# A hybrid decoder layer on one core: pages in VectorE's waits, a third sequence's values on VectorE, norm sums as float32r products, weight loads by groups

## The chip, the core and the metric

The kernel runs on one core of a Trainium2 chip. The metric is device time in microseconds (us), the median of repeated runs. TensorE multiplies matrices, VectorE and ScalarE work elementwise, GpSimd takes small elementwise work, SyncE issues DMAs. ScalarE's queue issues DMAs too.

## What is computed

One inference step of one layer. 512 prompt tokens, 16 meta tokens and 8 new tokens of 8 running sequences are normed and projected by one weight matrix, `w_in` (2048 x 8192). Its columns feed 8 heads of a gated recurrence (HGRN2) and 8 heads of differential attention. Each head's output is normed over its 128 values and gated, and `w_out` (2048 x 2048) maps the result back. The 8 new tokens also attend to 2048 cached positions each, in 16 pages of 128 rows for keys and 16 for values per sequence:

```python
z = rmsnorm(h, norm_g) @ w_in                    # split into hq, hf, hi, hg, aq, ak, av, ag
# new tokens: for each of 8 sequences, over 16 pages
s = einsum('bqhcd,bkhcd->bchqk', q, k) * 64 ** -0.5 + bias   # c = 0, 1: two key halves of 64
p = softmax(s); w = p[:, 0] - lam * p[:, 1]
o_at = einsum('bhqk,bkhv->bqhv', w, v)
# merge
mixed = concat(rmsnorm(o_hg) * silu(hg), rmsnorm(o_at) * silu(ag))
y = rmsnorm(h + mixed @ w_out)
```

Everything is float32, outputs included.

## The kernel before

**Projections.** The weights go through in 80 blocks of 128 columns, 64 of `w_in` (aq, ak, av, then hi/hf/hq by heads, hg, ag) and 16 of `w_out`. A block is four groups (`NG = 4`), each of four 128x128 weight tiles (`GK = 4`), so there are 320 groups, numbered u. Each operand is kept as two float32r parts: ScalarE casts the weights to `hi`, VectorE subtracts to get `lo` (`split`, L322). A group is 24 products on TensorE (`group`, L337): hi by xh, hi by xl and lo by xh, for two halves of the tokens, accumulated in `ps`. `split(u + LEAD)` runs three groups ahead; `hi` and `lo` have four buffers each, `ps` three.

**Weight loads.** `load_raw` (L314) loads half a block, 512 KB, into one of three `raw` buffers. After the first three, ScalarE's queue issues them, at every second group, behind that group's `hi` cast; the buffer must have been read by the `lo` of an earlier group.

**Around the groups.** The loop over u (L1317) emits `split`, `group`, then at a block's end `block_done` (ScalarE evacuates `ps`), then one step of each waiting thread: `attn` (L910), `hgrn` (L998), `norm_chain` (L875) for a head's norm, `softmax_dec` (L777) for the weights of one sequence, and so on. Then `value_step` and `fill`. Everything is recorded by `Counted`, so that all calls show line L151 and are best told apart by tiles. Each engine runs its own queue in the order in which the calls are emitted.

**Pages.** `page_step` (L675) does one half of a key page on VectorE: a product with the query (`pgt<-pgt,qb`), then a sum by heads (`scd<-pgt`). 128 key pages go before the last values may. Values of sequences 0 to 5 are weighted on TensorE (`value_step`, L702): eight steps for a sequence, each two pages, four products `t_pv<-pgt,wd`, added up on VectorE (`acc`). Sequences 6 and 7 (`ONV`, L282) go on VectorE (`dve_value_step`, L733): eight fused multiply-adds `qb<-pgt,wd,qb` for a page, and at the end two products with a matrix of ones on TensorE (`pv_sum`, L761).

**What sets the order.** `Clock` keeps an estimate of each engine's time while the program is written. `fill` (L603) emits page steps as long as VectorE's estimate is less than TensorE's plus `LATE`, which depends on the phase (before values, attention, recurrence, after):

```python
LATE, SOON = (3.0, 1.5, 4.0, 4.0), 0.0
while clock["dve"] < clock["pe"] + LATE[ph]:
    ...
    if not page_step() and not dve_value_step():
        break
```

At group 253 the program stops emitting groups until all norms and all values are done (L1327); any step that is still left stands there, between two groups.

**Norms of a head.** `norm_chain` squares a head's 512 tokens on ScalarE, sums over the partitions by one float32 product with ones (`t_ra` for attention, `t_rh` for the recurrence; 16 in all), and scales. The `tp` buffers of PSUM, two of them, are shared by nearly all of TensorE's small work.

**DMAs.** The DMAs of both issuing queues take eight completion semaphores (DMAHW0 to DMAHW7) in turn. A DMA whose semaphore is still in use by the DMA eight before it waits for that one to land, in its issuing queue.

Of the kernel before, what the change touches and what calls it, by code (L numbers as in the profile page):

```python
# [18 lines left out]
P = 128  # L19
D = 2048  # L20
# [55 lines left out]
class Clock:  # L76
# [30 lines left out]

    def issue(self, e, cost, outs, ins, latency=0.08, shared=False):
        start = self.now[e]
        for table, aps in ((self.written, ins + outs), (self.read, outs)):  # L110
            for ap in aps:
                t, by = table.get(ap.tensor.name, (0.0, e))
                if by != e:
                    start = max(start, t + self.LATENCY)
        if e == "pool":
            start = self.port(start)
            self.pool_held = start + cost
        elif shared:
            start = max(start, self.pool_held)
            a, b = self.held[-1]  # L120
            self.held = self.held[-40:]
            if start - b < 0.03:
                self.held[-1] = (a, start + cost)
            else:
                self.held.append((start, start + cost))
        self.now[e] = end = start + cost
        end += latency
        for ap in ins:
            n = ap.tensor.name
            self.read[n] = max(self.read.get(n, (0.0, "")), (end, e))  # L130
        for ap in outs:
            self.written[ap.tensor.name] = end, e
# [7 lines left out]

class Counted:


    def __init__(self, eng, clock, name):
        self.eng, self.clock, self.name = eng, clock, name

    def __getattr__(self, op):
        f = getattr(self.eng, op)

        def call(*a, **k):  # L150
            r = f(*a, **k)  # L151
            aps = [x for x in a if hasattr(x, "free_size")]
            outs = [x for x in (k.get("out"), k.get("accum_out")) if x is not None]
            if "out" not in k:
                outs.append(aps.pop(0))
            ins = aps + [x for n, x in k.items() if hasattr(x, "free_size") and n not in ("out", "accum_out")]
            n = max(ins[0].free_size(), 1) if op == "tensor_reduce" else (outs[-1] if "out" not in k else outs[0]).free_size()
            late, shared = 0.08, False
# [39 lines left out]
def layer_kernel(ctx: ExitStack, tc: tile.TileContext, A):  # L198
# [67 lines left out]
    load_x(1)  # L266
    ones = cp.tile([P, P], F32, name="ones")
    G.memset(ones, 1.0)
    eps = cp.tile([P, 1], F32, name="eps")
# [11 lines left out]
    NKB, NPB = 3, 2  # L281
    ONV = (6, 7)  # L282
    NG = KC // GK
    LEAD = 3

# [28 lines left out]
    def load_raw(i):  # L314

        b, z = divmod(i, 2)
        if b < NB:
            raws[i] = wp.tile([P, KC // 2, P], F32, name="raw", tag="raw", bufs=3)
            clock.arrive(raws[i], 0.5)
            (store if i > 2 else load)(out=raws[i], in_=blocks[b][1][z * D // 2:(z + 1) * D // 2, :].rearrange("(k p) n -> p k n", p=P))  # L320

    def split(u):  # L322

        if u >= NB * NG:
            return
        b, g = divmod(u, NG)
        i, z = divmod(u, NG // 2)
        raw = raws[i][:, z * GK:(z + 1) * GK, :]
        hi = clock.tile(wp.tile([P, GK, P], F32R, name="hi", tag="hi", bufs=4), "hi", 4)
# [3 lines left out]
        parts[u] = (hi, lo)  # L333
        if z == 0 and i:
            load_raw(i + 2)

# [17 lines left out]

    load_raw(0)


# [27 lines left out]

    load_x(2)
    load_raw(1)
    load_x(3)
    load_raw(2)
    norm_stat(4)  # L390
# [160 lines left out]

    for g in range(NG):
        split(NG + g)
# [27 lines left out]
    def flag(name):  # L581
        flags[name] = slot[0]
# [17 lines left out]

    LATE, SOON = (3.0, 1.5, 4.0, 4.0), 0.0

    def fill():  # L603

        ph = 0 if "av0" not in flags else 1 if "attn7" not in flags else 2 if "hgrn7" not in flags else 3
        while clock["dve"] < clock["pe"] + LATE[ph]:
            if turn_v[0] and dve_value_step():
                turn_v[0] = 0
                continue
            i = done[0]  # L610
            if i < len(kloaded) and any(clock.written[t.tensor.name][0] > clock["pe"] + SOON for t in (kloaded[i], qbs[ksteps[i][0]])):
                if not dve_value_step():
                    break
                continue
            turn_v[0] = 1
            if not page_step() and not dve_value_step():
                break

# [208 lines left out]
    def decode_q():  # L827
# [9 lines left out]
        load_values()  # L837
        flag("q")
        yield

# [34 lines left out]
    def norm_chain(o, n, g, name, sq=None):  # L875

        if sq is None:
            sq = hw.tile([P, 512], F32, name="sq", tag="t6")[:, :n]
        S.activation(sq, o, AF.Square)
        yield  # L880
        t = tp("t_" + name)
        T.matmul(t[:, :n], ones, sq, start=True, stop=True)
        S.activation(sq, t[:, :n], AF.Ln, scale=1.0 / P, bias=eps)
# [26 lines left out]
    def attn():  # L910
        live = {}
        for n in range(4 * H + 4):
# [53 lines left out]
            if i2:  # L966
# [5 lines left out]
                V.tensor_scalar(r[:, 1:2], r[:, 1:2], nlam, None, op0=ALU.mult)  # L972
                S.activation(p1[:, :L1], p1[:, :L1], AF.Copy, scale=r[:, 1:2])
            fill()
            if i2:
                V.scalar_tensor_tensor(p0[:, :L1], p0[:, :L1], r[:, 0:1], p1[:, :L1], op0=ALU.mult, op1=ALU.add)
            if n < 4 * H:
# [427 lines left out]
```

## Time and profile before

| | us |
|---|---|
| median of 3 runs | 1261.57 (1259.65 to 1262.13) |
| the profiled execution | 1256.73 |
| its span in the trace | 1254.9 |
| TensorE busy (matmuls) | 1214.3 |
| VectorE busy | 844.9 |
| ScalarE busy | 547.8 |

The granted clock averages 0.994 over the span. The span goes by stages: up to 40 us the prompt is normed and transposed, to 150 us groups alone, to 240 us groups beside key pages, to 450 us attention heads beside groups, to 880 us the recurrence, to 1020 us gates beside values, then `w_out`. A row of the list of waits names the instruction that waited, what it waited for, us in total, times and the longest. A row of the timeline gives start, duration, engine, line and operation, with the idle time before it in brackets.

### The profile page before, as it was taken

The page shows a single profiled execution, that of the slowest core. Times are in us where ns is not written, and L with a number is a line of the kernel's source. Part 1 is how long each engine was busy: PE and PEld are TensorE (multiplying, and loading weights), DVE is VectorE, ACT ScalarE, POOL GpSimd, SP SyncE. Part 2 cuts the span into 40 slices and gives each one's busy share as a digit, 9 for nine tenths or more (in the row PEclk, how much of TensorE's full clock was granted, in tenths as well). Part 3 has the DMA queues.
Part 4 walks back from the last instruction along what each step waited for, and adds up shares of the span by engine and source line. Part 5 has one row for each costly group of instructions (what it writes and reads, how often), then busy time and mean ns, then how long its engine had stood idle before and what let it go on. Part 6 is the DMA issues. An engine that isn't in the chain of part 4 may idle for free.

```text
span 1254.9 us, 24952 instructions
## 1 busy us (share of the span) xinstructions
PE 1214.3 (97%) x9412; PEld 1096.5 (87%) x9412; DVE 844.9 (67%) x1527; ACT 547.8 (44%) x1288; POOL 144.7 (12%) x151
## 2 busy tenths in 40 slices
PE   8999999999999999999998999999999999999995
PEld 6899999976777779888787888888999999999995
DVE  6522598865666578878668788888997936355253
ACT  6322323355555664545445455554432235223233
POOL 2000001100000001111012010122131410021020
PEclk9999999999999999999999999999999999999998
DMA  7353788935645576889796897987787636433223
GB/s 230 95 161 97 239 275 283 285 103 189 191 163 188 183 234 190 297 272 305 256 318 193 296 307 256 323 286 247 226 287 226 204 101 217 122 89 96 86 68 137
DMA packets 240956, 261.02 MB, mean 208 GB/s; under 512 B 8783, under 2 KB 198962, under 8 KB 240171
## 3 DMA queue, kind: packets, MB, share of 16 engines
q1 hardware_dynamic: 57298, 164.09, 37.5%
q10 hardware_dynamic: 183538, 95.34, 26.9%
q8 instruction: 74, 1.21, 0.4%
q14 instruction: 46, 0.38, 0.1%
HBM read 245.94 MB, written 16.14 MB: 209 GB/s over the span
## 4 chain that ended last, share of the span: by engine, by line
PE 86%; DVE 5%; DMA 4%; ACT 3%; issue 1%; ACTq 1%; SPq 0%; DVEq 0%
PE ps L151 69%; PE t_pv L151 4%; PE o L151 2%; PE ho L151 2%; PE sc L151 1%; DMA raw<-in_w_out 1%; DMA pgt<-in_cache_v 1%; DVE qb L151 1%; PE up L151 1%; PE t_w L151 1%; DVE lo L151 1%; PE at L151 1%; DVE scd L151 1%; PE t_ra L151 1%; PE t_y L151 1%
## 5 line engine op out<-in xcount | busy, mean ns | idle before, releaser
L151 PE MATMUL ps<-xh,hi 128*128 128x264 f32 (+2 forms) x2048 | 539.2, 294 | 3.9 <-ACT gate L151 2.2
L151 PE MATMUL ps<-xl,hi 128*128 128x264 f32 (+2 forms) x2048 | 521.8, 285 | 1.1 <-DVE xl L151 1.1
L151 PEld LDWEIGHTS ps<-xh,hi 128*128 128x128 f32 x2048 | 386.7, 189 | 58.2 <-issue 48.2
L151 PEld LDWEIGHTS ps<-xl,hi 128*128 128x128 f32 x2048 | 386.8, 189 | 2.6 <-issue 2.5
L151 DVE TENSOR_TENSOR lo<-raw,hi 128x512 fp32r<-128x512 f32 x321 | 244.1, 765 | 198.9 <-ACT hi L151 198.3
L151 PE MATMUL ps<-xh,lo 128*128 128x264 f32 (+2 forms) x2048 | 333.8, 285 | 0.0
L151 ACT CAST hi<-raw 128x512 fp32r<-128x512 f32 x321 | 196.3, 617 | 228.7 <-PE ps L151 187.5
L151 PEld LDWEIGHTS ps<-xh,lo 128*128 128x128 f32 x2048 | 284.6, 189 | 0.0
L151 DVE TENSOR_TENSOR pgt<-pgt,qb 128x1024 f32<-128x1024 f32 x128 | 163.7, 1279 | 14.5 <-DMA pgt<-in_cache_k 11.3
L151 DVE TENSOR_REDUCE scd<-pgt 128x16 f32<-128x1024 f32 x128 | 155.0, 1211 | 0.1
L151 PE MATMUL ps<-mh,hi 128*128 128x256 f32 (+1 forms) x512 | 130.0, 286 | 0.5 <-ACT y L151 0.5
L151 PE MATMUL ps<-ml,hi 128*128 128x256 f32 (+1 forms) x512 | 128.5, 283 | 0.0
L151 PEld LDWEIGHTS ps<-mh,hi 128*128 128x128 f32 x512 | 96.4, 188 | 1.0 <-ACT y L151 0.7
L151 PEld LDWEIGHTS ps<-ml,hi 128*128 128x128 f32 x512 | 96.5, 188 | 0.0
L151 PE MATMUL ps<-mh,lo 128*128 128x256 f32 (+1 forms) x512 | 82.5, 283 | 0.0
L151 DVE SCALAR_TENSOR_TENSOR qb<-pgt,wd,qb 128x128 f32<-128x128 f32 x240 | 70.9, 364 | 0.0
L151 PEld LDWEIGHTS ps<-mh,lo 128*128 128x128 f32 x512 | 70.3, 188 | 0.0
L151 PE MATMUL t_pv<-pgt,wd 128*32 128x512 f32 x384 | 53.9, 605 | 12.7 <-ACT wmT L151 4.2
L151 DVE SCALAR_TENSOR_TENSOR p<-p,r,p 128x144 f32<-128x144 f32 (+3 forms) x32 | 18.2, 568 | 71.3 <-ACT p L151 71.2
L151 DVE TENSOR_TENSOR acc<-acc,t_pv 128x512 f32<-128x512 f32 x42 | 28.7, 682 | 23.9 <-PE t_pv L151 23.9
L151 POOL TENSOR_TENSOR sd<-sd,vb 128x1024 f32<-128x1024 f32 x8 | 20.1, 2509 | 183.4 <-ACT vb L151 156.5
L151 ACT COPY hgm<-ho 128x128 f32<-128x128 f32 x32 | 8.5, 265 | 69.5 <-PE ho L151 59.6
(242 smaller groups left out, 1167.2 us busy)
## 6 DMA issues: line engine op xcount, KB each, us to landing
pgt<-in_cache_k SPq DMA_DIRECT2D x128, 512.0 KB
pgt<-in_cache_v SPq DMA_DIRECT2D x128, 512.0 KB
raw<-in_w_in ACTq DMA_DIRECT2D x125, 512.0 KB
raw<-in_w_out ACTq DMA_DIRECT2D x32, 512.0 KB
x<-in_x_prompt SPq DMA_DIRECT2D x4, 1024.0 KB
qb<-qd SPq DMA_DIRECT2D x8, 512.0 KB
sd<-in_state_hgrn SPq DMA_DIRECT2D x8, 512.0 KB
vb<-hvd SPq DMA_DIRECT2D x8, 512.0 KB
```

The costliest lines, as they stand in the source:

```text
L151: r = f(*a, **k)
```

## The change

- A VectorE instruction that would wait over 1 us by the estimate first lets page steps be emitted, as long as the wait lasts (`meanwhile`); `LATE` goes down in all four phases.
- Sequence 5's values are done on VectorE too (`ONV`).
- The 16 norms of heads: ScalarE squares into a `tp` buffer, casts to `sqh`, VectorE subtracts (`rest`), and two float32r products with ones replace the float32 one.
- Weights are loaded by groups of 256 KB into five buffers, one load at each group.
- In attention, the scaling of the second softmax half (`p<-p,r`) goes from ScalarE to VectorE, behind `fill`.
- The ones are cast to float32r on GpSimd at the start; one split that was done twice is done once.

```diff
--- before.py
+++ after.py
@@ Clock, Counted @@
+    def ready(self, e, outs, ins):
+
+        start = 0.0
         for table, aps in ((self.written, ins + outs), (self.read, outs)):
...
+        return start
+
+    def issue(self, e, cost, outs, ins, latency=0.08, shared=False):
+        start = max(self.now[e], self.ready(e, outs, ins))
...
 class Counted:
+    WAIT = 1.0
...
+            if self.meanwhile:
+                step, self.meanwhile = self.meanwhile, None
+                while self.clock.ready(self.name, outs, ins) - self.clock[self.name] > self.WAIT and step():
+                    pass
+                self.meanwhile = step
+            r = f(*a, **k)
@@ layer_kernel @@
-    ones = cp.tile([P, P], F32, name="ones")
-    G.memset(ones, 1.0)
+    ones_f = hw.tile([P, P], F32, name="ones_f", tag="ones")
+    G.memset(ones_f, 1.0)
+    ones_r = cp.tile([P, P], F32R, name="ones")
+    G.tensor_copy(ones_r, ones_f)
+    ones = ones_r.bitcast(F32)
...
-    ONV = (6, 7)
+    ONV = (5, 6, 7)
     NG = KC // GK
+    NRAW = 5
@@ load_raw, split @@
-        b, z = divmod(i, 2)
+        b, z = divmod(i, NG)
         if b < NB:
-            raws[i] = wp.tile([P, KC // 2, P], F32, name="raw", tag="raw", bufs=3)
-            clock.arrive(raws[i], 0.5)
-            (store if i > 2 else load)(out=raws[i], in_=blocks[b][1][z * D // 2:(z + 1) * D // 2, :].rearrange("(k p) n -> p k n", p=P))
+            raws[i] = wp.tile([P, GK, P], F32, name="raw", tag="raw", bufs=NRAW)
+            clock.arrive(raws[i], 0.25)
+            (store if i >= NRAW else load)(out=raws[i], in_=blocks[b][1][z * GK * P:(z + 1) * GK * P, :].rearrange("(k p) n -> p k n", p=P))
...
-        raw = raws[i][:, z * GK:(z + 1) * GK, :]
+        raw = raws.pop(u)
...
         S.copy(hi, raw)
         V.tensor_tensor(lo, raw, hi.bitcast(F32), op=ALU.subtract)
         parts[u] = (hi, lo)
-        if z == 0 and i:
-            load_raw(i + 2)
+        if u:
+            load_raw(u + NRAW - 1)
...
-    for g in range(NG):
+    for g in range(LEAD):
         split(NG + g)
@@ fill @@
-    LATE, SOON = (3.0, 1.5, 4.0, 4.0), 0.0
+    LATE, SOON = (2.0, 0.0, 0.5, 3.0), 0.0
+
+    def page(at):
+
+        if turn_v[0] and dve_value_step():
+            turn_v[0] = 0
+            return True
+        i = done[0]
+        if i < len(kloaded) and any(clock.written[t.tensor.name][0] > at for t in (kloaded[i], qbs[ksteps[i][0]])):
+            return dve_value_step()
+        turn_v[0] = 1
+        return page_step() or dve_value_step()
...
+        while clock["dve"] < clock["pe"] + LATE[ph] and aside(lambda: page(clock["pe"] + SOON)):
+            pass
@@ decode_q @@
         flag("q")
+        V.meanwhile = lambda: page(clock["dve"] + 0.3)
@@ norm_chain @@
-            sq = hw.tile([P, 512], F32, name="sq", tag="t6")[:, :n]
-        S.activation(sq, o, AF.Square)
-        yield
-        t = tp("t_" + name)
-        T.matmul(t[:, :n], ones, sq, start=True, stop=True)
+            rest = hw.tile([P, 512], F32R, name="rest", tag="t6")
+            hi = hw.tile([P, 512], F32R, name="sqh", tag="t7")
+            t = tp("t_sq")
+            S.activation(t, o, AF.Square)
+            S.copy(hi, t)
+            V.tensor_tensor(rest, t, hi.bitcast(F32), op=ALU.subtract)
+            yield
+            t = tp("t_" + name)
+            T.matmul(t, ones_r, hi, start=True, stop=False)
+            T.matmul(t, ones_r, rest, start=False, stop=True)
+            sq = hw.tile([P, 512], F32, name="sq", tag="t6")
...
@@ attn @@
-                S.activation(p1[:, :L1], p1[:, :L1], AF.Copy, scale=r[:, 1:2])
             fill()
             if i2:
+                V.tensor_scalar(p1[:, :L1], p1[:, :L1], r[:, 1:2], None, op0=ALU.mult)
                 V.scalar_tensor_tensor(p0[:, :L1], p0[:, :L1], r[:, 0:1], p1[:, :L1], op0=ALU.mult, op1=ALU.add)
```

On TensorE, at groups 191 and 192 in the recurrence (`t_rh` is a head's norm sum, `t_pv` a value step, `ps` the groups' products). Before:

```order
L151 MATMUL ps<-xh_111,lo 128x264 x4
L151 MATMUL t_rh<-sq,ones 128x512
L151 MATMUL t_mx<-ident,mx 16x128
L151 MATMUL ps<-xh_112,hi 128x256
...
L151 MATMUL ps<-xh_112,lo 128x264 x4
L151 MATMUL t_pv<-pgt,wd 32x512 x4
L151 MATMUL ps<-xh_109,hi 128x256
```

Now:

```order
L168 MATMUL ps<-xh_115,lo 128x264 x4
L168 MATMUL t_rh<-sqh,ones 128x512
L168 MATMUL t_rh<-rest,ones 128x512
L168 MATMUL ps<-xh_116,hi 128x256
...
L168 MATMUL ps<-xh_116,lo 128x264 x4
L168 MATMUL ps<-xh_113,hi 128x256
L168 MATMUL ps<-xl_117,hi 128x256
```

The norm sum has become two products, and the value step behind the next group is gone.

On VectorE, in attention around group 83 (`p` are the softmax halves, `ISA p,nm` the score with its bias, `pgt` and `scd` a key page's two halves). Before:

```order
L151 TENSOR_TENSOR acc<-acc,t_pv 128x512
L151 TENSOR_TENSOR lo<-raw,hi 128x512
L151 RECIPROCAL r<-s_3672 128x2
L151 TENSOR_SCALAR r<-r,nlam 128x1
L151 SCALAR_TENSOR_TENSOR p_3961<-p_3961,r,p_3963 128x400
L151 ISA p_4129,nm<-sc,strip 128x144
```

Now:

```order
L168 TENSOR_TENSOR acc<-acc,t_pv 128x512
L168 TENSOR_TENSOR lo<-raw,hi 128x512
L168 TENSOR_TENSOR pgt<-pgt,qb 128x1024
L168 RECIPROCAL r<-s_3755 128x2
L168 TENSOR_SCALAR r<-r,nlam 128x1
L168 TENSOR_SCALAR p_4080<-p_4080,r 128x400
L168 SCALAR_TENSOR_TENSOR p_4078<-p_4078,r,p_4080 128x400
L168 ISA p_4273,nm<-sc,strip 128x144
```

Half a key page has come in ahead of the reciprocal, and the scaling of `p` behind it.

On ScalarE, at a head's value tokens near group 85 (`vtok` the tokens, `out_v` their stores, semaphores waited for in brackets). Before:

```order
L151 CAST hi<-raw 128x512
L151 COPY vtok<-t_vtok 24x128 [waits DMAHW4_49,DMAHW3_49,PE_49]
L151 COPY vtok<-t_vtok 128x512
L865 DMA out_v_prompt<-vtok 128x4x128 [waits DMAHW2_49,Activation_49]
L866 DMA out_v_prompt<-vtok 16x128 [waits DMAHW3_49]
```

Now:

```order
L168 CAST hi<-raw 128x512 [waits DMAHW3_49]
L336 DMA raw<-in_w_in 128x4x128 [waits DMAHW2_49,DVE_49]
L168 COPY vtok<-t_vtok 24x128 [waits PE_49]
L168 COPY vtok<-t_vtok 128x512
L890 DMA out_v_prompt<-vtok 128x4x128 [waits DMAHW4_49,Activation_49]
L891 DMA out_v_prompt<-vtok 16x128 [waits DMAHW6_49]
```

A weight load stands here now, with waits of its own for VectorE and for an earlier DMA.

## Rows read from the trace of the kernel before

**Rows 1.** The profile's page, part 1: busy time and share, by engine.

```profile
PE 1214.3 (97%) x9412; PEld 1096.5 (87%) x9412; DVE 844.9 (67%) x1527; ACT 547.8 (44%) x1288; POOL 144.7 (12%) x151
```

**Rows 2.** The list of waits of TensorE, the longest: us, times, longest.

```profile
PE t_pv L151 <- ACT wmT L151: 4.2, 6, 0.7
PE t_x L151 <- DVE x L151: 4.0, 5, 1.5
PE t_pv L151 <- DVE wd L151: 3.7, 1, 3.7
...
PE ps L151 <- ACT gate L151: 2.2, 3, 0.9
PE t_w L151 <- ACT vtok L151: 2.1, 6, 0.3
PE ps L151 <- ACT ak L151: 1.7, 1, 1.7
```

**Rows 3.** Windows: us, busy by engine, granted clock, DMA share, GB/s.

```profile
280.00:440.00 160.00, 153.69 (x1030) 114.69 (x1028) 99.42 (x272) 90.38 (x254) 3.78 (x21) 1.00 0.56 183
560.00:600.00 40.00, 38.33 (x294) 31.62 (x293) 32.74 (x44) 19.35 (x49) 4.81 (x4) 1.00 0.93 304
880.00:1000.00 120.00, 117.81 (x957) 114.98 (x956) 112.57 (x307) 41.09 (x74) 31.82 (x20) 1.00 0.76 242
```

**Rows 4.** Timeline of TensorE: value step, sums of values, norm sum, one group's end.

```profile
442.44 1.07 PE L151 MATMUL t_pv<-pgt,wd 128*32 128x512 f32 x8
443.43 0.39 PE L151 MATMUL ps<-xh,hi 128*128 128x272 f32 x1
...
474.68 0.64 PE L151 MATMUL ps<-xh,lo 128*128 128x256 f32 x4
475.17 0.28 PE L151 MATMUL ps<-xh,hi 128*128 128x264 f32 x1
...
505.50 1.02 PE L151 MATMUL t_rh<-sq,ones 128*128 128x512 f32 x2
506.45 1.07 PE L151 MATMUL t_pv<-pgt,wd 128*32 128x512 f32 x8
...
952.17 1.05 PE L151 MATMUL t_pv<-qb,ones 128*32 128x512 f32 x4
953.15 0.39 PE L151 MATMUL ps<-xh,hi 128*128 128x256 f32 x1
```

**Rows 5.** The page's part 5: groups of VectorE: busy us, mean ns | idle before.

```profile
L151 DVE TENSOR_TENSOR lo<-raw,hi 128x512 fp32r<-128x512 f32 x321 | 244.1, 765 | 198.9 <-ACT hi L151 198.3
L151 DVE TENSOR_TENSOR pgt<-pgt,qb 128x1024 f32<-128x1024 f32 x128 | 163.7, 1279 | 14.5 <-DMA pgt<-in_cache_k 11.3
L151 DVE SCALAR_TENSOR_TENSOR qb<-pgt,wd,qb 128x128 f32<-128x128 f32 x240 | 70.9, 364 | 0.0
L151 DVE SCALAR_TENSOR_TENSOR p<-p,r,p 128x144 f32<-128x144 f32 (+3 forms) x32 | 18.2, 568 | 71.3 <-ACT p L151 71.2
L151 DVE TENSOR_TENSOR acc<-acc,t_pv 128x512 f32<-128x512 f32 x42 | 28.7, 682 | 23.9 <-PE t_pv L151 23.9
```

**Rows 6.** VectorE's instructions on tile rfin: ns min/median/max, first and last start.

```profile
L151 DVE TENSOR_SCALAR xr<-xr,rfin x6: 478/482/488, 1237.5 to 1245.5; 128x512 f32<-128x512 f32 x6
```

**Rows 7.** Timeline near group 43, a block's end in the key stage.

```profile
164.02 1.22 DVE L151 TENSOR_TENSOR pgt<-pgt,qb 128x1024 f32<-128x1024 f32 x1
...
165.15 0.68 DVE L151 TENSOR_TENSOR lo<-raw,hi 128x512 fp32r<-128x512 f32 x1
...
165.87 0.40 ACTq L320 DMA_DIRECT2D raw<-in_w_in  x1
166.31 0.73 ACT L151 COPY ak<-ps 128x272 f32<-128x272 f32 x3 [4.58 <-DVE lo L151]
166.75 0.39 PE L151 MATMUL ps<-xh,hi 128*128 128x264 f32 x1 [1.72 <-ACT ak L151]
```

**Rows 8.** The list of waits, ScalarE for a DMA.

```profile
ACT hv L151 <- DMA pgt<-in_cache_v: 9.1, 1, 9.1
```

**Rows 9.** The page's parts 2 and 3: DMA tenths in 40 slices; queues' packets, MB, share.

```profile
DMA  7353788935645576889796897987787636433223
...
q1 hardware_dynamic: 57298, 164.09, 37.5%
q10 hardware_dynamic: 183538, 95.34, 26.9%
```

More of the change, by code (lines that the diff above doesn't have):

```diff
@@ L106, in port @@
         return t
-    def issue(self, e, cost, outs, ins, latency=0.08, shared=False):
-        start = self.now[e]
+    def ready(self, e, outs, ins):
+        start = 0.0
         for table, aps in ((self.written, ins + outs), (self.read, outs)):
@@ L141 @@
 class Counted:
+    WAIT = 1.0
     def __init__(self, eng, clock, name):
         self.eng, self.clock, self.name = eng, clock, name
+        self.meanwhile = None
     def __getattr__(self, op):
@@ L150, in call @@
         def call(*a, **k):
-            r = f(*a, **k)
             aps = [x for x in a if hasattr(x, "free_size")]
@@ L325, in split @@
             return
-        b, g = divmod(u, NG)
-        i, z = divmod(u, NG // 2)
-        raw = raws[i][:, z * GK:(z + 1) * GK, :]
+        raw = raws.pop(u)
         hi = clock.tile(wp.tile([P, GK, P], F32R, name="hi", tag="hi", bufs=4), "hi", 4)
@@ L355, in layer_kernel @@
     load_raw(0)
+    load_raw(1)
     xh = [big.tile([P, GK, CK], F32R, name=f"xh{g}", tag=f"xh{g}") for g in range(NG)]
@@ L386, in layer_kernel @@
     load_x(2)
-    load_raw(1)
+    load_raw(2)
+    load_raw(3)
     load_x(3)
-    load_raw(2)
+    load_raw(4)
     norm_stat(4)
@@ L599, in step_threads, with aside @@
         return ran
-    LATE, SOON = (3.0, 1.5, 4.0, 4.0), 0.0
+    LATE, SOON = (2.0, 0.0, 0.5, 3.0), 0.0
[8 more added lines that the diff above has]
+        return page_step() or dve_value_step()
     def fill():
         ph = 0 if "av0" not in flags else 1 if "attn7" not in flags else 2 if "hgrn7" not in flags else 3
[L606 to L617, printed above, removed]
+        while clock["dve"] < clock["pe"] + LATE[ph] and aside(lambda: page(clock["pe"] + SOON)):
+            pass
+    def aside(step):
+        keep, V.meanwhile = V.meanwhile, None
+        r = step()
+        V.meanwhile = keep
+        return r
     def later(slots, **k):
@@ L877, in norm_chain @@
         if sq is None:
-            sq = hw.tile([P, 512], F32, name="sq", tag="t6")[:, :n]
-        S.activation(sq, o, AF.Square)
-        yield
-        t = tp("t_" + name)
-        T.matmul(t[:, :n], ones, sq, start=True, stop=True)
+            rest = hw.tile([P, 512], F32R, name="rest", tag="t6")
[9 more added lines that the diff above has]
+            sq = hw.tile([P, 512], F32, name="sq", tag="t6")
+        else:
+            S.activation(sq, o, AF.Square)
+            yield
+            t = tp("t_" + name)
+            T.matmul(t[:, :n], ones, sq, start=True, stop=True)
         S.activation(sq, t[:, :n], AF.Ln, scale=1.0 / P, bias=eps)
```

## Prediction

> **What bounds the kernel now.** I read the busy times first: TensorE is busy 97% of the span, VectorE 67%, ScalarE 44% [rows 1]. Then the waits of TensorE: the longest kind is 4.2 us in six pieces, and the rows shown add up to 17.9 us of 1254.9 [rows 2]. So TensorE is the bound nearly all the way, and a change is worth what it takes from TensorE's queue, less what it adds of waits. The long waits of VectorE, 198.3 us for `hi` and 71.2 us for ScalarE's scaling of `p` [rows 5], cost nothing as such: VectorE is not the bound. They are room. The windows say where: in attention VectorE is busy 99.4 of 160 us, in the value stage 112.57 of 120 [rows 3]. The granted clock is 1.00 in these windows, the upper level of 2.4 GHz, and nothing here should lower it, since TensorE stays as busy as it was.
>
> **Values of sequence 5.** Removed from TensorE: eight value steps. One runs from 442.44 to the next product at 443.43, 0.99 us [rows 4]: 8 x 0.99 = 7.9 us. Added: one pair of sums with ones, 952.17 to 953.15, 0.98 us [rows 4]. The four transposes at a sequence's end exist either way, though narrower. Net -6.9 us. On VectorE 128 multiply-adds come in at 70.9/240 = 0.295 us, 37.8 us, and eight `acc` additions go at 28.7/42 = 0.68 us, 5.5 us [rows 5]: +32 us.
>
> **Norm sums.** One float32 product of 512 tokens runs from 505.50 to 506.45, 0.95 us [rows 4]. A float32r product of 512 columns doesn't exist before. The nearest row: four float32r products of 256 columns take 474.68 to 475.17, 0.49 us [rows 4], as many columns as two of 512. Bounds for the pair: 0.245 us, if the number of products counts and not their columns (2 x 0.49/4), and 0.95 us, if each of the two costs half of what they replace. I take 0.49, by columns, since the row is of the same kind of product. 16 x (0.95 - 0.49) = 7.4 us off. The first group product behind a float32 one starts its successor later: it shows 0.39 us where one inside a group shows 0.28 [rows 4], some 0.1 us. By the order, the eight `t_ra` stand between float32 products, so this switch is paid once more there, 0.8 us. Net -6.6 us, between +0.8 and -10.5.
>
> Beside it: ScalarE does one cast more for a chain, VectorE 16 subtractions at 0.765 us as for `lo` [rows 5], 12 us, and the square takes one of the two `tp` buffers until the subtraction is done. The next user of that buffer stands one iteration later on TensorE, more than 3 us on. I cost this at 0, with up to 0.5 us for each of 16 chains, 8 us, if VectorE is late.
>
> **Scaling of `p` on VectorE.** 32 instructions, at most as dear as 482 ns for 512 columns [rows 6], 15 us on VectorE, off ScalarE. The 71.2 us for which VectorE stood still for ScalarE [rows 5] go. TensorE waits for neither: 0.
>
> **Pages in waits, and LATE.** The order shows key pages ahead of waiting instructions from group 76 on. The last key page stands at group 193 where it stood at 209, so that the 48 value pages get groups 193 to 245; 32 had 209 to 241. The last sums stand behind group 246 instead of 243, the norm that needs them behind 249 instead of 246, and the stop is at 253, so nothing is left for the stop. In attention VectorE gets ten key pages more (two halves of about 1.2 us, of which the first is 1.279 [rows 5]), 25 us, and for six heads 24 scalings and six subtractions, 24 x 0.482 + 6 x 0.765 = 16 us: about 140 of 160 us, 88%. That fits.
>
> **Weight loads by groups.** 160 issues more on ScalarE's queue, 0.40 us each [rows 7], 64 us; ScalarE has 700 us idle [rows 1]. What counts is what a load waits for. Near group 43 VectorE did a page half at 164.02, `lo` only at 165.15, the load behind it at 165.87, and ScalarE's evacuation stood behind that load: 4.58 us for ScalarE, 1.72 for TensorE [rows 7]. Now a load stands at every group. At a block's end one stood already, so the evacuation gets no new wait for `lo` there; with the smaller `LATE`, VectorE should run ahead less, and I take half of the waits for `ak` and `gate` (3.9 us [rows 2]) as gone: -2. New are waits for DMAs: of ScalarE's DMAs from group 41 to 251, 13 wait for one that SyncE issues at most two groups earlier; now 38 do, ten of them one group earlier. In attention ScalarE idles behind its `hi` cast anyway, so most are covered; I take 0.1 us for each of the 25, +2.5. The loads are not dearer in themselves: the queue with the weights, q10, spends its time by packets (183538 of them, 26.9% of the engines [rows 9]), and each piece is still one weight row of 512 B.
>
> The Trainium skill, page DMA: Bandwidth & Descriptors, section Bandwidth, speaks against this part: transfers should be batched to 1 MiB or more, because each pays some 2 us that don't shrink with size. By its formula, an estimate, 512 KB take 3.2 us and two of 256 KB 5.2, 1.62 times as much; in the fullest window, where weights are a quarter of the traffic (below), that asks for 0.93 x 1.155 = 1.07 of the engines, 3 us in 40. By the rule the sum would be some 3 us worse, 1251.6. By the packets it is unchanged, and I follow the packets; no row of before shows a weight load of 256 KB.
>
> **The rest** costs nothing: the cast of the ones delays the first products by some 0.3 us, at a time at which TensorE waits for `x` [rows 2]; the double split was on engines with room. TensorE's waits in attention, for `wmT` and `vtok` (6.3 us [rows 2]), stay: its order there is the same row by row, but for the norm sums.
>
> **The sum.** -6.9 - 6.6 - 2 + 2.5 = -13.0 us on a span of 1254.9. The profiled execution took 1256.73, 1.8 more than its span, and the median 1261.57 is 4.8 above that; I carry both: 1261.57 - 13.0 = **1248.6 us**. The forecast's own range is 1242 to 1254 (norms 0 to -8, the `tp` buffer 0 to 8 in part).
>
> **Rivals.**
>
> *Waits go too.* If paging with less lateness takes all of the waits of rows 2 but those for `x` at the start, 13.9 us, of which 2 are counted already, another 11.9 us go: 1236.7. For it: the smaller `LATE`, the 3.7 us for `wd` [rows 2]. Against it: the 6.3 us in attention have another cause, the stores of `vtok` ahead of `wmT`.
>
> *ScalarE's queue is held up by the weight loads* (the slower side). Mechanism: a load that waits for VectorE or for an earlier DMA holds all that ScalarE has behind it, `wT` and `wmT` in attention, evacuations at a block's end. ScalarE's longest single hold for such a page DMA was 9.1 us [rows 8], and rows 7 show how 4.58 us on ScalarE become 1.72 on TensorE. With 25 close waits more, 13.5/25 = 0.54 us each on TensorE eats the gain; from there on it decides. At 1 us each: 1261.57 - 15.5 + 25 = 1271. For it: ten waits on a page issued only one group before, five of these in attention on weight loads, others on the stores of `vtok`, where nothing covers them. Against it: rows 8 is the one hold for a page in the list, though 13 such waits stood there, and TensorE's wait list has nothing of its size. The Trainium skill, same page, section Anatomy of one DMA, says that a DMA's semaphore waits are served on the issuing sequencer; rows 8 agree.
>
> *VectorE becomes the bound in the value stage.* 48 pages at 8 x 0.295 and 52 `lo` at 0.765 are 153 us of VectorE for 52 groups; a group is 24 products at 0.49/4, 2.94 us [rows 4], 153 us. Any more work makes it late. The order leaves four groups, 12 us, from the last norm to the stop; at 20 us of lateness TensorE loses 8: 1256.6. Against it: the pace of before was a page for each group, and 112.57 of 120 us busy were enough [rows 3].
>
> *DMA-bound.* If a load of half the size keeps the engines busy for more than half the time. In the window at 0.93 TensorE ran 294 products, at most 12 groups, 12 x 0.26 MB in 40 us: 79 of 304 GB/s, a quarter [rows 3]. Bounds: no dearer, and as dear as a whole load, 0.93 x 1.25 = 1.16. Four slices of 31.4 us show nine tenths or more [rows 9]: 0 to 4 x 31.4 x 0.16 = 20 us, 1248.6 to 1268.7; the middle is 1258.7. Against it: the packets, above.
>
> **How the numbers follow.** Forecast 0.58, waits go too 0.14, ScalarE's queue held 0.13, VectorE late 0.09, DMA-bound 0.06. The measurement tells 0.2%, 2.5 us, from no change, so faster is below 1259.0, slower above 1264.1. Faster: 0.58 + 0.14, 0.07 of VectorE late, 0.02 each of the held queue and of DMA-bound: 0.83. Same: 0.02 + 0.02 + 0.03 = 0.07. Slower: 0.09 of the held queue and 0.01 of DMA-bound, 0.10. The range 1236 to 1262 leaves out the held queue's slower part, the upper end of DMA-bound and half of the case in which the waits go, 0.18.
>
> **What would show it.** `t_pv<-pgt,wd` x320 instead of x384, `t_pv<-qb` x12, pairs of `t_ra`/`t_rh` 0.4 to 0.5 us long; TensorE's busy time about 13 us lower; VectorE's wait for `p` gone and the one for `hi` much smaller; VectorE near 900 us. Wrong would be: a float32r product of 512 columns at 0.4 us or more; waits of TensorE for ScalarE (`wmT`, `ak`, `gate`, `hgm`) that grow past 15 us together, with ScalarE held by a DMA or by `lo`; a gap of TensorE behind group 253.

## The result and the profile after

The changed kernel takes **1247.2 us** (median of 4 executions, 1242.77 to 1247.67) beside 1261.85 of the kernel before on the same chip: a ratio of 0.9876, interval 0.9849 to 0.9904. Run again with more executions it is 1247.7 and 0.9895 (0.9875 to 0.9916). That is faster, by 13 to 16 us, and the forecast of 1248.6 is 1.4 us off. The sum was right. The experiments below show that several of its terms were not.

The profiled execution took 1246.93 us with a span of 1244.9; its busy times (us, share of the span, number) and the queue of the weights (packets, MB, share of the DMA engines' time) answer rows 1 and 9:

```profile
PE 1203.6 (97%) x9352; PEld 1096.7 (88%) x9352; DVE 910.7 (73%) x1693; ACT 542.6 (44%) x1272; POOL 145.4 (12%) x152
...
q10 hardware_dynamic: 186578, 95.61, 26.8%
```

TensorE lost 10.7 us of work and is still the bound at 97%. VectorE took 66 us more and, at 73%, is not the bound. The queue with the weights, q10, carries twice the loads for the same share of the engines.

The list of TensorE's waits (us in total, times, longest) answers rows 2:

```profile
PE t_pv L168 <- ACT wmT L168: 4.9, 6, 1.0
PE t_pv L168 <- DVE rest L168: 4.1, 2, 2.6
...
PE t_rh L168 <- DVE rest L168: 2.1, 2, 1.6
PE ho L168 <- DVE am L168: 2.1, 1, 2.1
PE t_w L168 <- ACT vtok L168: 2.1, 6, 0.3
...
PE ps L168 <- ACT ak L168: 1.3, 1, 1.3
...
PE t_ra L168 <- DVE rest L168: 1.2, 2, 0.7
```

The waits for `wd` (3.7) and `gate` (2.2) are gone, those for `wmT` and `vtok` stayed. New are three rows for `rest`, VectorE's subtraction in the norm sums: 4.1 + 2.1 + 1.2 = 7.4 us.

Two of VectorE's groups answer rows 5 (busy us, mean ns, idle before):

```profile
L168 DVE TENSOR_TENSOR lo<-raw,hi 128x512 fp32r<-128x512 f32 x320 | 254.7, 801 | 202.5 <-ACT hi L168 202.2
...
L168 DVE SCALAR_TENSOR_TENSOR p<-p,r,p 128x528 f32<-128x528 f32 x8 | 7.1, 882 | 0.3
```

The 71.2 us of waiting for ScalarE's `p` are gone (0.3 in each of the four shapes). The wait for `hi` did not shrink, 202.2 after 198.3.

And the granted clock, by windows (us, busy by engine TensorE first, clock, DMA share, GB/s):

```profile
360.00:400.00 40.00, 37.94 (x243) 28.18 (x244) 27.76 (x74) 19.82 (x58) 1.77 (x4) 0.91 0.64 200
400.00:440.00 40.00, 38.76 (x255) 28.72 (x254) 36.11 (x83) 22.69 (x62) 1.63 (x5) 0.96 0.64 207
416.00:420.00 4.00, 3.10 (x16) 0.92 (x13) 3.82 (x14) 2.42 (x8) 0.00 (x0) 0.69 0.89 282
680.00:720.00 40.00, 40.00 (x307) 35.91 (x304) 33.73 (x49) 18.24 (x51) 5.68 (x5) 0.96 0.92 301
840.00:880.00 40.00, 37.92 (x300) 36.05 (x298) 35.30 (x112) 22.74 (x52) 5.33 (x6) 0.96 0.74 250
1000.00:1040.00 40.00, 40.00 (x328) 38.81 (x327) 22.62 (x53) 21.12 (x41) 8.86 (x6) 1.00 0.30 86
```

Before, one stretch fell below the upper level of 2.4 GHz while TensorE had work, behind the 3.7 us for `wd`; now five do, two of them in 360 to 400. What they cost is estimated as 1 less the clock, times the window: 3.6 us in 360 to 400, 1.6 in 400 to 440, 1.6 each in 680 to 720 and in 840 to 880, 8.4 us. Before it was 1.6, in 680 to 720. TensorE's busy time holds most of this, so at the full clock it fell by about 10.7 + 6.8 = 17.5 us. The last row is the stop at group 253: no gap. These are two executions; the executions differ in their clock, as the next section shows.

### The profile page after: what moved, and what is told of

It is laid out like the page before. It is cut to its first block, busy times and chain, and to the rows that moved or that the text cites. A ratio compares the mean times of both kernels' runs of the same rounds, so it can differ in the third digit from the quotient of the medians.

```text
span 1244.9 us, 25324 instructions
## 1 busy us (share of the span) xinstructions
PE 1203.6 (97%) x9352; PEld 1096.7 (88%) x9352; DVE 910.7 (73%) x1693; ACT 542.6 (44%) x1272; POOL 145.4 (12%) x152
## 3 DMA queue, kind: packets, MB, share of 16 engines
q10 hardware_dynamic: 186578, 95.61, 26.8%
## 4 chain that ended last, share of the span: by engine, by line
PE 81%; DVE 10%; DMA 3%; ACT 3%; issue 2%; ACTq 1%; SPq 0%; DVEq 0%
PE ps L168 68%; PE t_pv L168 3%; DVE scd L168 2%; DVE pgt L168 2%; PE ho L168 1%; DMA pgt<-in_cache_v 1%; DVE lo L168 1%; DMA raw<-in_w_in 1%; PE sc L168 1%; PE o L168 1%; PE up L168 1%; DVE p L168 1%; PE t_w L168 1%; PE at L168 1%; PE t_y L168 1%
## 5 line engine op out<-in xcount | busy, mean ns | idle before, releaser
L168 DVE TENSOR_TENSOR lo<-raw,hi 128x512 fp32r<-128x512 f32 x320 | 254.7, 801 | 202.5 <-ACT hi L168 202.2
L168 DVE TENSOR_TENSOR pgt<-pgt,qb 128x1024 f32<-128x1024 f32 x128 | 155.8, 1217 | 11.9 <-DMA pgt<-in_cache_k 10.6
L168 DVE SCALAR_TENSOR_TENSOR qb<-pgt,wd,qb 128x128 f32<-128x128 f32 x360 | 104.1, 363 | 1.2 <-DMA pgt<-in_cache_v 1.2
L168 PE MATMUL t_pv<-pgt,wd 128*32 128x512 f32 x320 | 47.9, 639 | 10.9 <-ACT wmT L168 4.9
L168 ACT ACTIVATE p<-p,nm 128x144 f32<-128x144 f32 (+3 forms) x64 | 36.2, 566 | 1.9 <-DVE nm L168 1.9
L168 DVE TENSOR_TENSOR xr<-xr,t_y 128x512 f32<-128x512 f32 (+1 forms) x17 | 11.2, 657 | 31.1 <-PE t_y L168 31.1
```

## The experiments

Each kernel has its ratio to the kernel before on the same chip. A difference between two kernels is that of their ratios times 1262 us; its "either way" is the root of the summed squares of the two half intervals.

### The changed kernel again

> The changed kernel once more, beside the three that follow, so that they share one chip. Both theories: about 1247 us, 0.988 of the time before. Its trace should again hold short stretches of the granted clock at 0.5 behind waits of TensorE, but not at the same places.

1247.7 us, 0.9895 (0.9875 to 0.9916). Its executions show how the clock and the time go together: 1246.85 at a mean granted clock of 0.990, 1251.41 at 0.985; of the first set, 1242.77 at 0.993.

In its trace the falls of the clock stand, as expected, at other places, near 154, 287 and 509 us, and only the last, near 861, where one stood. In 680 to 720, behind the same wait of 2.55 us for `rest`, the clock holds (timeline, then window):

```profile
680.88 1.07 PE L168 MATMUL t_pv<-pgt,wd 128*32 128x512 f32 x8 [2.55 <-DVE rest L168]
...
680.00:720.00 40.00, 39.12 (x309) 34.37 (x310) 35.25 (x52) 18.23 (x51) 5.52 (x5) 1.00 0.96 319
```

### One part undone: sequence 5's values

```diff
-    ONV = (5, 6, 7)
+    ONV = (6, 7)
```

> Sequence 5's values back on TensorE, all else as changed. Theory (TensorE's own work sets the time): eight value steps come back at 0.99 us and one pair of sums goes, +6.9 us, about 1254. Rival (VectorE is now so full that its lateness costs TensorE, in the waits for rest): 32 us of VectorE go, the 7 us of waits for rest and the clock's short falls go with them, and the time stays at about 1247 or falls.

1258.15 us, 0.9968 (0.9952 to 0.9984). The part is worth 9.2 us, about 3.3 either way; 6.9 had been forecast. That is more than the theory's 1254 us and far from the rival's 1247.

### One part undone: the norm sums

```diff
-            t = tp("t_sq")
-            S.activation(t, o, AF.Square)
-            S.copy(hi, t)
-            V.tensor_tensor(rest, t, hi.bitcast(F32), op=ALU.subtract)
...
-            T.matmul(t, ones_r, hi, start=True, stop=False)
-            T.matmul(t, ones_r, rest, start=False, stop=True)
+        S.activation(sq, o, AF.Square)
...
+        T.matmul(t[:, :n], ones, sq, start=True, stop=True)
```

> The 16 norm sums as one float32 product again, all else as changed. Theory (TensorE's own work): a pair of float32r products measured about 0.46 us against 0.95 for the float32 one, so +7 us less the 0.8 for the switch, about 1253. Rival (the waits for rest, 7.4 us in the profiled execution, eat what the shorter products give): about 1247.

1243.34 us, 0.986 (0.9834 to 0.9885): without its norm part the change is 4.4 us faster, about 4.1 either way. The rival is right: the saving is given back, and, just clear of the interval, somewhat more.

Windows (us, TensorE's busy time, clock, DMA share, GB/s), first of the changed kernel, then of this one:

```profile
320.00:460.00 140.00, 134.63 (x891) 0.96 0.63 202
...
700.00:1000.00 300.00, 295.42 (x2386) 0.99 0.74 234
```

```profile
320.00:460.00 140.00, 134.53 (x906) 1.00 0.66 212
...
700.00:1000.00 300.00, 299.74 (x2421) 1.00 0.72 226
```

TensorE idles 0.3 us of 300 in the later stage instead of 4.6, and in both stretches the clock holds. Over the two whole traces, without the norm part TensorE works about 8.9 us more at the full clock (1205.8 us busy less 1.7 for one fall, near 157 us, against 1203.6 less 8.4), stands 6.5 us less (34.8 of 1240.6 against 41.3 of 1244.9) and loses about 6.7 us less to the clock: 4.3 us shorter. The executions without a trace agree on the clock: its mean is 0.993 in the six of this kernel and 0.989 in the ten of the changed one, some 5.5 us. How the new sum waits is in the changed kernel's timeline around 677 us (start, us, engine, instruction, wait):

```profile
676.21 0.61 ACT L168 ACTIVATE t_sq<-hgm 128x512 f32<-128x512 f32 x1
676.36 0.28 PE L168 MATMUL t_mx<-ident,mx 128*16 128x128 f32 x1 [0.26 <-ACT oSh L168]
676.72 1.22 DVE L168 TENSOR_TENSOR pgt<-pgt,qb 128x1024 f32<-128x1024 f32 x1
...
677.86 0.69 DVE L168 TENSOR_TENSOR lo<-raw,hi 128x512 fp32r<-128x512 f32 x1
678.46 0.68 DVE L168 TENSOR_TENSOR rest<-t_sq,sqh 128x512 fp32r<-128x512 f32 x1
...
679.20 1.07 PE L168 MATMUL t_pv<-pgt,wd 128*32 128x512 f32 x8 [2.55 <-DVE rest L168]
...
680.48 0.42 PE L168 MATMUL ps<-xl,hi 128*128 128x256 f32 x1
```

The squares sit in one of the two `tp` buffers from 676.21, `t_mx` has the other. The value step `t_pv`, which has nothing to do with the norm, needs the first and gets it when `rest` is done at 679.14. On VectorE a page half and a `lo` stand ahead of `rest`. TensorE waits 2.55 us, and the products behind run at the lower level of 1.2 GHz: 0.42 us where one takes 0.28 at the upper level.

### The second product left out

Only the float32r part of the squares is summed here; the rest is computed and not used.

```diff
-            T.matmul(t, ones_r, hi, start=True, stop=False)
-            T.matmul(t, ones_r, rest, start=False, stop=True)
+            T.matmul(t, ones_r, hi, start=True, stop=True)
```

> The changed kernel without the second product of the norm sums: VectorE still subtracts the rest of the squares, but TensorE sums only their float32r part, so the small part of the norm is left out of the result. Theory (the float32r pair saves work on TensorE, but the subtraction on VectorE that stands between, 7.4 us of waits for rest, and the clock falls behind such waits give the gain back): the waits for rest go (7.4 us), 16 products of about 0.23 us go (3.7 us), one or two of the clock falls of 1.7 us go: 1247.5 - 11 to -14 = 1234 to 1237 us, idle time inside TensorE's work near 21 us. Rival (the wait for rest only stands where TensorE would wait for ScalarE's squares or for the next tile anyway): only the products go, 1244.

1249.35 us (1239.21 to 1253.76), 0.9883 (0.9847 to 0.9919): 1.5 us below the changed kernel, about 5 either way, so no gain that can be measured. My theory's 11 us or more failed; the rival's 3.5 us, the products alone, lies within the interval. Rows of its waits, and one window:

```profile
PE t_pv L168 <- DVE rest L168: 4.1, 2, 2.6
...
PE t_ra L168 <- DVE rest L168: 1.5, 2, 0.8
```

```profile
460.00:700.00 240.00, 230.21 (x1778) 0.98 0.85 281
```

Of 7.4 us for `rest`, 5.6 stay: TensorE waits less for the operand than for the buffer that `rest` sets free. And the clock is lower still, 0.98 over these 240 us. Five executions have a mean clock of 0.984 or 0.985 and take 1249 to 1254 us; one has 0.994 and takes 1239.21, which is 3.6 below the changed kernel's 1242.77 at 0.993. That would fit a gain from the product left out that the clock takes back in the other five; two single executions on two chips do not settle it.

### The products moved one step later

```diff
             V.tensor_tensor(rest, t, hi.bitcast(F32), op=ALU.subtract)
-            yield
+            yield 2
```

> The changed kernel with the norm's products one iteration later, so that VectorE has a group more for the subtraction. Theory (TensorE's waits for rest are lateness of VectorE by less than a group): 7 us of waits for rest go, and a fall of the clock or two: about 1239. Rival (the square still holds one of the two tp buffers, and TensorE waits for the same subtraction through the buffer, in t_pv): about 1247, with the waits under t_pv or t_w.

1253.72 us, 0.9915 (0.9883 to 0.9947): not faster: 2.5 us slower, about 5 either way. From its list of waits:

```profile
PE ps L168 <- ACT ak L168: 3.2, 1, 3.2
PE t_sum L168 <- ACT sqs L168: 2.9, 1, 2.9
PE t_pv L168 <- DVE rest L168: 2.6, 1, 2.6
```

The wait for the operand `rest` in `t_rh` is gone; one for the buffer stays, and `sqs` comes in; `ak` is 1.3 and 2.6 us in the two traces of the changed kernel, so its 3.2 says little. The clock is 0.95 in 320 to 460. The longest wait for the buffer is as long as before: more distance between a subtraction and its product does not free the buffer sooner.

### One part undone: pages in VectorE's waits

```diff
-        V.meanwhile = lambda: page(clock["dve"] + 0.3)
...
-    LATE, SOON = (2.0, 0.0, 0.5, 3.0), 0.0
+    LATE, SOON = (3.0, 1.5, 4.0, 4.0), 0.0
```

> No pages in VectorE's waits, LATE as before (3.0, 1.5, 4.0, 4.0), all else as changed. By the order the last value page then stands at group 252 and the last sums and the norm behind them at the stop, group 253. Theory (paging gives nothing on TensorE itself; it makes room so that a third sequence fits ahead of the stop): TensorE stands at the stop for the sums, copies, transposes and the norm, some 8 to 15 us, 1255 to 1262, with one gap behind group 253. Rival (paging takes waits away all along): the same or more, but spread, and without a gap at the stop. Second rival (paging costs as much as it gives): 1247.

1266.52 us, 1.0039 (1.0022 to 1.0056): 18 us slower than the changed kernel and slower than the kernel before. Its longest wait, its only one for `rest`, and VectorE's timeline at the stop up to 1040 us:

```profile
PE t_pv L168 <- DVE qb L168: 23.0, 1, 23.0
...
PE t_pv L168 <- DVE rest L168: 1.6, 1, 1.6
```

```profile
1024.87 15.30 DVE L168 SCALAR_TENSOR_TENSOR qb<-pgt,wd,qb 128x128 f32<-128x128 f32 x58
```

Values on VectorE reach the stop (ten pages, 80 multiply-adds in all, to 1045.9 us), and TensorE stands for 23 us. The theory named the place; the gap is longer than its 8 to 15 us. So the paging makes the room for the third sequence. What it is worth beside that no run shows. It also has a price: without it the waits for `rest` are 1.6 us instead of 7.4, which speaks for pages drawn in ahead as what makes the subtraction late.

### One part undone: the scaling of `p`

```diff
+                S.activation(p1[:, :L1], p1[:, :L1], AF.Copy, scale=r[:, 1:2])
             fill()
             if i2:
-                V.tensor_scalar(p1[:, :L1], p1[:, :L1], r[:, 1:2], None, op0=ALU.mult)
```

> The changed kernel with the scaling of p by r back on ScalarE, as before; all else as changed. VectorE loses 72 operations of about 0.4 us (30 us) and gets back the wait for ScalarE's p (71 us before), into which it now draws page work. In this kernel's order the sequences' values end at group 251 and the last sums stand at the stop, not at 243 and 249 as in the changed kernel. Theory (VectorE's hidden work has little slack left, so the queue decides): TensorE waits a few us for qb at the stop, 1250 to 1256 us. Rival (hidden, p scaling is worth nothing as it was costed): 1246 to 1249.

1246.48 us, 0.9871 (0.9841 to 0.99): the same as the changed kernel within about 4.5 us, though its values end at group 251. VectorE waits for ScalarE's `p` again, 44.9 us of it now instead of 71.2:

```profile
DVE lo L168 <- ACT hi L168: 179.1, 110, 4.8
DVE p L168 <- ACT p L168: 44.9, 30, 3.8
```

The theory fell, the part is worth nothing that can be measured. (VectorE loses 32 operations and 11.3 us, not the 72 and 30 of the expectation.) The two rows also say why the mark on `hi` was wrong: VectorE is not the bound, so work put into one wait lets another grow, 179.1 and 44.9 here where the changed kernel has 202.2 and next to nothing.

### One part alone: the loads by groups

```diff
-            raws[i] = wp.tile([P, KC // 2, P], F32, name="raw", tag="raw", bufs=3)
-            clock.arrive(raws[i], 0.5)
+            raws[i] = wp.tile([P, GK, P], F32, name="raw", tag="raw", bufs=NRAW)
+            clock.arrive(raws[i], 0.25)
...
-        if z == 0 and i:
-            load_raw(i + 2)
+        if u:
+            load_raw(u + NRAW - 1)
...
```

The kernel before with these loads, and with the split that was done twice done once; 315 loads instead of 157.

> The kernel before with the weights' loads by groups of 4 rows of tiles (five buffers of half the size, twice the loads), as the changed kernel has them; nothing else. Theory (the packets are the same and the queue's share of the DMA engines stayed at 26.9 and 26.8%, and close waits for the loads cost next to nothing): within 2 us of the kernel before, 1260 to 1263.5. Rival (the fixed part of 40 more loads shows on ScalarE's queue, as I costed it): +2.5, 1264 us; and rival on the other side (raw tiles land a microsecond sooner and some waits for hi go): 1258 or less.

1252.71 us, 0.991 (0.988 to 0.994): 11.4 us faster, about 3.8 either way. Theory and first rival both fell. A window of this kernel; then the waits in which ScalarE's copies out of PSUM and its outputs stood behind VectorE's `lo` or a weight load, of this kernel and, in the last fence, of the kernel before:

```profile
460.00:700.00 240.00, 238.27 (x1870) 1.00 0.86 285
```

```profile
ACT y L151 <- DVE lo L151: 7.7, 3, 2.7
...
ACT ak L151 <- DVE lo L151: 4.9, 1, 4.9
...
ACT hv L151 <- DVE lo L151: 4.3, 1, 4.3
...
ACT ktok L151 <- DVE lo L151: 3.0, 1, 3.0
...
ACT gate L151 <- DMA raw<-in_w_in: 1.9, 1, 1.9
ACT gate L151 <- DVE lo L151: 1.4, 1, 1.4
```

```profile
ACT ak L151 <- DVE lo L151: 13.6, 5, 4.6
...
ACT hgm L151 <- DMA raw<-in_w_in: 9.8, 2, 5.5
...
ACT gate L151 <- DVE lo L151: 7.4, 2, 3.7
...
ACT y L151 <- DVE lo L151: 5.1, 2, 2.5
```

These add up to 23.2 us, and to 35.9 before: ScalarE stands less behind `lo` and the loads. TensorE shows it less clearly: its wait for `wd` with the fall of the clock behind it is gone (238.27 us busy of 240 in 460 to 700, 232.71 before), and a wait of 3.1 us for `gate` comes in near 895 us. The two profiled executions differ by 4.9 us only, so more than half of the 11.4 lies in executions without a trace. The order moved with it (by the count of `lo`, VectorE's values stand some three groups earlier, at 204 to 237, since the planner's times are other ones); how much of the gain is that, and how much the loads themselves, is open. The planner's times change in the other experiments too, so each measures its edit with the order that comes of it.

### The stores of the value tokens later

In attention ScalarE issues three stores of `vtok` and a weight load before it copies `wmT`, for which TensorE waits. Here the stores are queued for a later step.

```diff
+        put = (lambda **k: later(1, **k)) if name == "vtok" else store
-        store(out=dst[0, 0, NM:NKEY, h, :].rearrange("(j p) d -> p j d", p=P), in_=tok[:, 0:4, :])
+        put(out=dst[0, 0, NM:NKEY, h, :].rearrange("(j p) d -> p j d", p=P), in_=tok[:, 0:4, :])
...
```

On the changed kernel:

> The changed kernel with the three stores of a head's value tokens issued one iteration later, behind ScalarE's copies wT and wmT. Theory (TensorE's waits for vtok and wmT, 2.1 and 4.9 us in six heads, come from those issues in ScalarE's queue, and the granted clock falls behind the longest of these waits): the 7 us go, and with them three falls of 3.4 us at 0.5, 1.7 us each, up to 5: about 1236 to 1240. Rival (ScalarE is late there by its own work, or the first wait, for vtok itself, stays): under 3 us of gain, 1245.

1241.78 us, 0.9843 (0.9819 to 0.9868), 6.6 us below the changed kernel, about 4 either way; the theory asked for 7.5 to 11.5. On the kernel before:

> The kernel before, with the value tokens' stores one iteration later. Theory: the 6.3 us of waits for wmT and vtok go here too, about 1255 (0.995), so the waits are older than the change. Rival (they come from ScalarE's own work): 1262.

1255.65 us, 0.9955 (0.9936 to 0.9973): 5.7 us, about 2.3 either way. In both, `t_pv` no longer waits for `wmT` (in the changed kernel `t_ra` and `t_sum` do, 1.3 us together), and the 2.1 us for `vtok` stay. So these waits are older than the change and none of its doing, and their 4.2 us lie within what the edit gained.

With the later products as well:

> Both of these. If each takes its own waits away, the gains add: about 1231 to 1235. If waits only move to the next late engine, about as much as the better of the two.

1245.05 us, 0.9857 (0.9827 to 0.9886): no better than the later stores alone (1241.78; 1.8 us slower, about 4.8 either way).

### A better version

The changed kernel with the old norm sums and the later stores.

> The changed kernel with both of the edits that each made it faster by itself: the norm sums as before (one float32 product of 512 columns) and the stores of the value tokens held back behind the keys' work. Theory (the two gains are of different waits, ScalarE's wmT waits of 4.8 us here and the waits for rest with the clock falls there, so they add): 1243.3 - 5.9 = 1237.4 us, between 1235 and 1240, t_pv<-ACT wmT gone from TensorE's waits, idle time inside TensorE's work near 17 us (22.1 with the old norm alone), at most 2 stretches at the lower clock. Rival (a wait that goes in one place comes back in another, since TensorE, ScalarE and VectorE are coupled by the hand-over of small tiles): 1242 to 1244, no better than the better of the two alone.

**1238.01 us** (1236.61 to 1239.51), 0.9802 (0.9778 to 0.9826): the gains add, and this beats both kernels. Beside the later stores alone the old norm sums gain 5.2 us, about 4.3 either way: the second pair that says so. In this pair the mean clock hardly differs (0.994 and 0.993), so here the clock does not seem to carry it. The waits for `rest` and those of `t_pv` for `wmT` are gone; behind `x` at the start, the longest is now:

```profile
PE ps L168 <- ACT ak L168: 3.1, 1, 3.1
```

## Why the prediction was right, and where it was not

In brackets stands the half interval; minus is faster.

| step | forecast, us | measured, us | by |
|---|---|---|---|
| values of sequence 5 | -6.9 | -9.2 (3.3) | undone |
| norm sums | -6.6 | +4.4 (4.1), +5.2 (4.3) | undone, on two kernels |
| scaling of `p` | 0 | +3.0 (4.5) | undone |
| pages and LATE | -2 | -18 (3.3), in this kernel | undone |
| loads by groups | +2.5 | -11.4 (3.8) | alone |
| all | -13.0 | -15.6 (3.5), -13.2 (2.6) | the two sets |

**Right by two errors that cancel, which is luck.** The total is 1.4 us off. The norm sums are 11 us worse than their term and the loads 14 us better. Values, norms and loads as measured give -9.2 + 4.4 - 11.4 = -16.2, near the whole. But the parts were measured on different kernels: no run undoes the loads in the changed kernel, so that they are worth 11.4 us there is not shown. The -18 for paging is not added, since it is the room in which the -9.2 stand.

**Values of sequence 5: right.** `t_pv<-pgt,wd` x320 and `t_pv<-qb,ones` x12 are there, and the size is within the interval.

**Norm sums: the price was nearly right, the wait was not.** TensorE's timeline (start, us) shows first the pair in the changed kernel and the next product, then the float32 product in the kernel with the old norm sums and its successors:

```profile
511.95 0.39 PE L168 MATMUL t_rh<-sqh,ones 128*128 128x512 f32 x1
512.18 0.40 PE L168 MATMUL t_rh<-rest,ones 128*128 128x512 f32 x1
512.42 0.29 PE L168 MATMUL ps<-xh,hi 128*128 128x272 f32 x1
```

```profile
579.74 1.02 PE L168 MATMUL t_rh<-sq,ones 128*128 128x512 f32 x2
580.20 0.68 PE L168 MATMUL ps<-xh,hi 128*128 128x256 f32 x1
580.72 0.28 PE L168 MATMUL ps<-xl,hi 128*128 128x256 f32 x1
580.83 0.28 PE L168 MATMUL ps<-xh,hi 128*128 128x256 f32 x1
```

From 511.95 to 512.42 are 0.47 us, where 0.49 was taken by the columns. The float32 product and its first successor take 0.98 us (to 580.72), and 0.87 without the successor's own 0.11 (580.72 to 580.83): 0.40 saved where 0.46 was counted. (In attention, where 0.36 was left for each, a pair of `t_ra` mostly takes 0.66 up to the next product instead of 1.06, 0.40 too.) What failed is the step "I cost this at 0, with up to 0.5 us for each of 16 chains, 8 us, if VectorE is late". It was late: 7.4 us of waits for `rest`, near that upper bound, more than the whole saving, 16 x 0.40 = 6.4. With the clock, below, that makes the loss; how the two share it is open, since only one of the five falls stands behind a wait for `rest`. Squares kept out of the `tp` buffers would test the wait by itself; no run does that. And "the next user of that buffer stands one iteration later on TensorE, more than 3 us on" was wrong: the value step above would have started at 679.20 - 2.55 = 676.65, 0.4 us behind the start of the squares.

**The clock was left out.** The forecast said that "nothing here should lower it, since TensorE stays as busy as it was". The busy share did stay at 97%, and the clock fell five times instead of once, 6.8 us more. That is most of what lies between TensorE's 17.5 us of work saved (of which values and norm sums, 6.9 + 6.4, explain 13.3) and the 10.0 us by which the two spans differ. The profiled execution of before was a good one: over 49 executions of before the mean clock is 0.992, over the ten of the changed kernel 0.989, which is some 4 us.

**Pages and LATE: right in the mechanism.** Values end before the stop, no gap behind group 253, the waits for `gate` are gone (2.2) and those for `ak` went from 1.7 to 1.3, or 2.6 in the second trace; with paging undone they are 2.0 and 2.1. That is near the forecast's -2. That paging also carries the values' gain was not said, nor that its pages could delay `rest`; without it the values' gain becomes a stop of 23 us.

**Loads by groups: wrong in sign.** The close DMA waits that were to cost 2.5 us show nowhere: TensorE's waits for `wmT`, `ak`, `gate` and `hgm` are 4.9 + 1.3 = 6.2 us, below the 15 that were named as the mark, and the rival in which the loads hold ScalarE's queue did not come. That ScalarE stands less behind `lo` and the loads (23.2 us instead of 35.9 in the kernel with this part alone) was in the sum with 2 us at most. That this is what gives the 11.4 us is likely, not shown. By the rule of the Trainium skill (DMA: Bandwidth & Descriptors, section Bandwidth) this part would have been 3 us worse; its 2 us for each DMA and the formula stand in that page's section Anatomy of one DMA, fitted to DMAs that GpSimd issues, while ScalarE issues these. The queue's share is 26.8% after 26.9%, and the run is 11.4 us faster, so here the measurement decides against it.

**Other marks.** VectorE's 910.7 us is near the 900 named, and its wait for `p` is gone as said. That the wait for `hi` would be "much smaller" was wrong. Of the rivals, VectorE as the bound of the value stage did not come with paging (TensorE is busy 40.00 us of 40 around the stop) and came in full without it. The waits did not go either: `wd` and `gate`, 5.9 us, left, `rest` and `am`, 9.5 us, came. DMA as the bound did not come: in the stretches of 40 us in which the engines are busiest, 160 to 200 and 520 to 560 with 0.96 and 0.95, TensorE is busy 40.00 us. Two slips in the working change nothing: rows 9 show five slices at nine tenths, not four, so that rival reaches 25 us and not 20; and the gain that the held queue would eat is 13.5 us at one place and 15.5 at the next, 0.54 or 0.62 us a wait.

## What to carry to other kernels

A cheaper product is worth its saving only if its operands are ready: ask which shared buffer the new intermediate result holds, until which busy engine lets go of it, and who needs that buffer next, even if it belongs to other work. Room on an engine that is not the bound can be used, but the use and what makes the room (here a third sequence and paging) are one edit, and undone alone either looks like a large loss. And a right total doesn't confirm its terms: undo each part before keeping it, since one part of this change costs some 4 to 5 us.

## What was not expected of the hardware

TensorE's granted clock fell behind short waits. In the changed kernel the window 416 to 420 shows 0.69 behind a wait of 0.90 us for `wmT`, behind 2.55 us for `rest` the products of the timeline above take 0.42 us instead of 0.28, and 840 to 880, in which the wait of 2.1 us for `am` lies, shows 0.96. It isn't every such wait: the same program, run again, waits 2.55 us for `rest` and keeps 1.00 in 680 to 720, and the kernel with the old norm sums waits as long for `wmT` (4.8 us in six, 1.1 the longest) and keeps 1.00 in 320 to 460. What tells them apart is open. The executions of the changed kernel and of several variants differ mostly by this: 1239.21 us at a mean clock of 0.994 and 1253.76 at 0.984 of one and the same program, the one without the second product. In the kernel before the clock explains less: at 0.993 its executions on one chip take 1256.04 to 1265.21 us. So what lowers the clock belongs in a sum like the one above.
